# Low parts of weights: a subtraction on VectorE against a negated copy on ScalarE and an accumulating transfer

## The chip, the cores and the metric

The kernel runs on one core of a Trainium2 chip. The metric is the device time of one execution in microseconds (us), the median of the runs shown.

## The reference, cut to what matters

Two layers of a streaming encoder are computed for 512 prompt tokens and 64 sample tokens. Each layer has a combined input projection that feeds a gated convolution, two kinds of attention and three gates, a merge, an output projection, cross-attention into 256 memory tokens, and a gated MLP with a depthwise convolution:

```python
def layer(x, pos, lp, hist, mem_k, mem_v):
    g = lp['g_norms']
    m, new = token_mixers(rmsnorm(x, g[0]), pos, lp, hist)
    x = x + rmsnorm(m, g[1])
    c = cross_attention(rmsnorm(x, g[2]), mem_k, mem_v, lp['w_ca_q'], lp['w_ca_o'])
    x = x + rmsnorm(c, g[3])
    f, ffn_state = conv_ffn(rmsnorm(x, g[4]), lp['w_up'], lp['ffn_conv_w'], lp['w_down'], hist['ffn'])
    x = x + rmsnorm(f, g[5])
```

All inputs are float32. D_MODEL is 1024, D_FF is 2816.

## The kernel before, in words

Activations are held with features on the 128 partitions and the 576 tokens along the free dimension, in two halves of 288 (`HALF`). Every float32 operand of a matrix product is split into a high part (rounded to fp32r) and a low part (what the rounding left), and a product is three fp32r matmuls: high by high, low by high, high by low (`mm3`, L152). PE therefore runs three matmuls per tile of 128 by 128 weights and half of the tokens.

Weights come from memory through `load_w` (L137). It takes up to 1024 columns at a time into a buffer `raw` (three buffers of 1024 columns, `RAW` = 3), a load issued on SP (L143). For each piece of 512 columns or less it takes a pair of tiles, `wh` and `wl` (ten of each, `WH` = 10). ScalarE (ACT) copies the raw weight into `wh` with rounding (L130, by the helper at L123), and VectorE (DVE) writes raw minus high into `wl` (L131, by the helper at L126). There are 674 such pieces in the program. Nearly all dense products use a tile of 1024 columns, which is two pieces, eight steps of 128 along the contraction; 48 matmuls use it. The down projection (`down`, L1246) runs in five stages per layer, of four or five steps; its tiles have 512 or 640 columns, so that a five-step tile is one full piece and one of 128 columns.

The order of the instructions on each engine is written by a scheduler when the program is built, and each engine then executes its own list in that order. POOL holds the squares of the first norm (L227), the sums of the merge (L1086), half of the sums of squares (L243), the reciprocal square roots of the norms (L276), the residual sums (L329), the small copies of the convolution's edges (L951, L952, L955, L956) and a few transfers. DVE holds the evacuations of PSUM that are multiplied by something, the conv taps, and the low parts. ACT holds the plain evacuations, exponentials, squares, the Gelu, and the high parts.

The program begins with the input norm, the memory keys and values of both layers, and the cached latents (`begin`, L958), then goes through forgetting attention, latent attention, merge, cross-attention and MLP of layer 0, and the same of layer 1.

Of the kernel before, what the change touches and what calls it, by code (L numbers as in the profile page):

```python
# [15 lines left out]
F32 = mybir.dt.float32  # L16
F32R = mybir.dt.float32r
BF16 = mybir.dt.bfloat16
AF = mybir.ActivationFunctionType
ALU = mybir.AluOpType  # L20
# [4 lines left out]
P = 128  # L25
# [10 lines left out]
CONV_AT = {11: (0,), -1: (1,), 0: (2,), 2: (3,)}  # L36
ORDER = "xwh0ltcbnLmM"
GEARLY, FEARLY = 3, 2
RAW, WH = 3, 10
LAT_AT, MEM_AT = (1,), ((0, 1), (), ())  # L40
STAGES, NACT = ((0, 4), (4, 9), (9, 14), (14, 18), (18, 22)), 14
APOOL, XPOOL, OPOOL = (0, 1, 2, 3), (0, 1, 2, 3, 4), (0, 1, 2, 3, 4)
# [19 lines left out]
class Kernel:  # L62
# [74 lines left out]
    def load_w(self, ap, cols):  # L137

        pieces = []
        for c0 in range(0, cols, 1024):  # L140
            n0 = min(1024, cols - c0)
            raw = self.raw.tile([P, 1024], F32, tag="raw", name="raw")
            self.nc.sync.dma_start(raw[:, :n0], ap[:, c0:c0 + n0])  # L143
            for c in range(0, n0, 512):
                n = min(512, n0 - c)
                hi = self.wp.tile([P, 512], F32R, tag="wh", name="wh")
                lo = self.wp.tile([P, 512], F32R, tag="wl", name="wl")
                self.split(hi[:, :n], lo[:, :n], raw[:, c:c + n])
                pieces.append((hi, lo))
        return Weights(pieces)  # L150

# [1337 lines left out]
```

## Time and profile before

| what | us |
|---|---|
| median of two runs | 2537.87 (2537.53 to 2538.21) |
| the profiled execution, its own time | 2537.41 |
| its span, first to last instruction | 2535.3 |

The profile is of one execution. PE is TensorE's matmuls, PEld its weight loads, DVE is VectorE, ACT ScalarE, POOL GpSimd, SP SyncE. A line such as L123 is often a helper's, so the tile names say which of its uses is meant. "Idle before" is the time an engine stood still just ahead of a group, with what ended it. DMA shares are the mean busy share of the 16 DMA engines.

### The profile page before, as it was taken

How to read it: one execution, taken by the hardware profiler on the slowest of the kernel's cores; microseconds unless marked ns; L12 is line 12 of the kernel's file. 1: busy time of each engine (PE TensorE's matmuls, PEld its weight loads, DVE VectorE, ACT ScalarE, POOL GpSimd, SP SyncE). 2: the span in 40 equal slices, each digit the busy share in tenths (PEclk: the TensorE clock that was granted, in tenths of full speed). 3: DMA queues.
4: the chain of work that ended last, by engine and by line, in shares of the span. 5: the costliest groups of instructions: out<-in, count | busy, mean ns of one | idle time of the engine just before them, and what ended most of it. 6: DMA issues, size and time to landing. Idle time of an engine off the chain costs nothing. (4 is left out here: it accounts for less than half of the span.)

```text
span 2535.3 us, 45273 instructions
## 1 busy us (share of the span) xinstructions
PE 2418.0 (95%) x17478; PEld 2320.8 (92%) x17478; DVE 1576.6 (62%) x3249; ACT 1143.4 (45%) x2479; POOL 403.6 (16%) x723
## 2 busy tenths in 40 slices
PE   6999999999999999999989999999999899999997
PEld 6888897899998899999987889889999889999997
DVE  7757768644436675566676677774453767566565
ACT  4556545533345543333345554553233564433332
POOL 4000021002221421011130001100121323101012
PEclk9999999999998899999988999999999999999998
DMA  6763143333222032322233223323233202222321
GB/s 226 233 188 98 59 134 100 113 102 102 84 98 90 28 101 63 101 71 84 78 98 103 96 71 108 121 89 122 88 103 113 87 23 87 86 90 62 93 84 52
DMA packets 97510, 249.10 MB, mean 98 GB/s; under 512 B 12520, under 2 KB 26920, under 8 KB 97104
## 3 DMA queue, kind: packets, MB, share of 16 engines
q1 hardware_dynamic: 88880, 230.67, 29.4%
q0 software_dynamic: 3296, 8.54, 1.2%
q10 hardware_dynamic: 5120, 7.00, 0.8%
q8 instruction: 138, 2.26, 0.4%
q14 instruction: 76, 0.62, 0.1%
HBM read 206.18 MB, written 30.94 MB: 94 GB/s over the span
## 5 line engine op out<-in xcount | busy, mean ns | idle before, releaser
L123 ACT ACTIVATE wh<-raw 128x512 fp32r<-128x512 f32 (+2 forms) x674 | 405.1, 612 | 663.3 <-PE ps_S L156 300.9
L126 DVE TENSOR_TENSOR wl<-raw,wh 128x512 fp32r<-128x512 f32 (+2 forms) x674 | 444.7, 668 | 251.8 <-ACT wh L123 239.6
L155 PE MATMUL ps_d<-hh,wh 128*128 128x288 f32 (+1 forms) x1672 | 503.9, 301 | 0.8 <-DVE qbd L135 0.5
L157 PE MATMUL ps_d<-hh,wl 128*128 128x288 f32 (+1 forms) x1672 | 503.1, 301 | 0.0
L156 PE MATMUL ps_d<-hl,wh 128*128 128x288 f32 (+1 forms) x1672 | 502.1, 300 | 0.0
L156 PE MATMUL ps_S<-hl,wh 128*128 128x288 f32 (+1 forms) x1256 | 372.7, 297 | 0.4 <-DVE hl L285 0.4
L155 PE MATMUL ps_S<-hh,wh 128*128 128x288 f32 (+1 forms) x1256 | 371.7, 296 | 1.2 <-ACT hh L123 1.2
L157 PE MATMUL ps_S<-hh,wl 128*128 128x288 f32 (+1 forms) x1256 | 371.7, 296 | 0.0
L155 PEld LDWEIGHTS ps_d<-hh,wh 128*128 128x128 f32 (+1 forms) x1672 | 319.2, 191 | 3.3 <-issue 1.4
L157 PEld LDWEIGHTS ps_d<-hh,wl 128*128 128x128 f32 (+1 forms) x1672 | 319.0, 191 | 1.6 <-DVE wl L126 0.3
L156 PEld LDWEIGHTS ps_d<-hl,wh 128*128 128x128 f32 (+1 forms) x1672 | 319.2, 191 | 1.3 <-issue 0.2
L155 PEld LDWEIGHTS ps_S<-hh,wh 128*128 128x128 f32 (+1 forms) x1256 | 235.5, 188 | 2.8 <-ACT hh L123 1.8
L156 PEld LDWEIGHTS ps_S<-hl,wh 128*128 128x128 f32 (+1 forms) x1256 | 235.5, 187 | 1.5 <-DVE hl L285 0.6
L157 PEld LDWEIGHTS ps_S<-hh,wl 128*128 128x128 f32 (+1 forms) x1256 | 235.1, 187 | 0.6
L1086 POOL TENSOR_TENSOR mf<-mf,tm 128x288 f32<-128x288 f32 x64 | 64.4, 1006 | 451.4 <-DVE tm L1085 451.4
L955 POOL COPY fst<-u 128x2 f32<-128x2 f32 x88 | 32.2, 366 | 472.6 <-DVE u L319 472.6
L155 PE MATMUL ps_S<-ah,wh 128*128 128x288 f32 x352 | 105.6, 301 | 0.4 <-DVE m L1257 0.4
L156 PE MATMUL ps_S<-al,wh 128*128 128x288 f32 x352 | 105.8, 301 | 0.0
L157 PE MATMUL ps_S<-ah,wl 128*128 128x288 f32 x352 | 105.1, 299 | 0.0
L155 PE MATMUL ps_d<-ah,wh 128*128 128x288 f32 x352 | 104.0, 295 | 1.0 <-ACT ah L123 0.9
L157 PE MATMUL ps_d<-ah,wl 128*128 128x288 f32 x352 | 103.9, 295 | 0.0
L156 PE MATMUL ps_d<-al,wh 128*128 128x288 f32 x352 | 103.9, 295 | 0.0
(500 smaller groups left out, 5810.5 us busy)
## 6 DMA issues: line engine op xcount, KB each, us to landing
raw<-in_w_dram SPq DMA_DIRECT2D x250, 512.0 KB
raw<-in_down_dram SPq DMA_DIRECT2D x48, 256.0 KB
raw<-in_down_dram SPq DMA_DIRECT2D x32, 320.0 KB
of<-o_scr SPq DMA_DIRECT2D x24, 288.0 KB
x<-in_xT_dram SPq DMA_DIRECT2D x16, 288.0 KB
o_scr<-of SPq DMA_DIRECT2D x16, 288.0 KB
raw<-in_ukv_dram SPq DMA_DIRECT2D x8, 512.0 KB
kc_scr<-k SPq DMA_DIRECT2D x8, 512.0 KB
```

The lines of the kernel that those rows point to most:

```text
L123: self.nc.scalar.activation(out, in_, func, scale=scale, **k)
L126: self.nc.vector.tensor_tensor(out, a, b, op=ALU.subtract)
L155: mm(ps, w[0], x[0], start=first, stop=False)
L156: mm(ps, w[0], x[1], start=False, stop=False)
L157: mm(ps, w[1], x[0], start=False, stop=last)
L955: self.nc.gpsimd.tensor_copy(dst[:, 0:2], u[:, 512:514])
L1086: nc.gpsimd.tensor_tensor(mf[j][:, a:b], mf[j][:, a:b], tm[:, a:b], op=ALU.add)
```

## The change

`load_w` no longer fills a buffer of 1024 columns for two pieces. Each piece of up to 512 columns has a buffer of its own (tag `neg`, four of them) and a load of its own. ACT writes the negated, rounded weight into `wl` and the rounded weight into `wh`. Then a transfer issued on POOL adds the raw weight to `wl` in SBUF, element by element. DVE has no part in it. `RAW` goes from 3 to 1: the buffer of 1024 columns stays for two small constant loads. In SBUF the raw buffers take 12 KB per partition before and after.

```diff
-RAW, WH = 3, 10
+RAW, WH = 1, 10
...
         for c0 in range(0, cols, 1024):
             n0 = min(1024, cols - c0)
-            raw = self.raw.tile([P, 1024], F32, tag="raw", name="raw")
-            self.nc.sync.dma_start(raw[:, :n0], ap[:, c0:c0 + n0])
             for c in range(0, n0, 512):
                 n = min(512, n0 - c)
                 hi = self.wp.tile([P, 512], F32R, tag="wh", name="wh")
                 lo = self.wp.tile([P, 512], F32R, tag="wl", name="wl")
-                self.split(hi[:, :n], lo[:, :n], raw[:, c:c + n])
+                raw = self.raw.tile([P, 512], F32, tag="neg", name="raw", bufs=4)
+                self.nc.sync.dma_start(raw[:, :n], ap[:, c0 + c:c0 + c + n])
+                self.act(lo[:, :n], raw[:, :n], scale=-1.0)
+                self.act(hi[:, :n], raw[:, :n])
+                self.nc.gpsimd.dma_start(lo[:, :n], raw[:, :n].bitcast(F32R), accum_op=ALU.add)
                 pieces.append((hi, lo))
```

Two lines are added ahead of most of the file, so L276 of before is L278 after, and so on. The order of the instructions changes on every engine. Three places show it.

POOL at the start of the program, before. `sq` and `acc` are squares of the input and their sums, `r` is the reciprocal root of a norm, `mt` the memory tokens:

```order
L227 TENSOR_TENSOR acc<-x 128x288
L227 TENSOR_TENSOR sq<-x 128x288 x7
L276 TENSOR_TENSOR r<-s,negh 96x3
L227 TENSOR_TENSOR sq<-x 128x288 x5
L384 TENSOR_TENSOR acc<-mt 128x256
```

and after:

```order
L229 TENSOR_TENSOR acc<-x 128x288
L229 TENSOR_TENSOR sq<-x 128x288 x4
L150 DMA wl<-raw 128x320
L229 TENSOR_TENSOR sq<-x 128x288 x3
L278 TENSOR_TENSOR r<-s,negh 96x3
L150 DMA wl<-raw 128x512 x3
L229 TENSOR_TENSOR sq<-x 128x288 x4
L386 TENSOR_TENSOR acc<-mt 128x256
```

The accumulating transfers stand among the squares of the first norm.

POOL in the merge of layer 0, where `mf` is the merged sum and `pacc` a sum of squares. Before:

```order
L897 DMA vs<-vc_scr_108 128x1024
L1086 TENSOR_TENSOR mf<-mf,tm 128x288 x32
L243 TENSOR_TENSOR pacc<-pacc,sq 128x288 x7
```

and after (the pattern goes on to the end of the merge):

```order
L1047 DMA out_conv_dram<-cst 128x16
L150 DMA wl<-raw 128x512 x31
L1088 TENSOR_TENSOR mf<-mf,tm 128x288 x2
L150 DMA wl<-raw 128x512 x3
```

Three transfers now stand between two pairs of sums.

ACT in the MLP of layer 0, from the end of one pair of up tiles into the first stage of the down projection; `ah` is the activated product, `y` the conv output, `m` the output of the down projection. Before:

```order
L123 ACTIVATE ah<-at 128x576
L123 ACTIVATE wh<-raw 128x512 x2
L123 ACTIVATE y<-u,fprm 128x578
L123 ACTIVATE wh<-raw 128x512 x2
L123 ACTIVATE y<-y 128x578
L123 ACTIVATE y<-u,fprm 128x578
L123 ACTIVATE m<-ps_d 128x288
```

and after:

```order
L123 ACTIVATE ah<-at 128x576
L123 ACTIVATE wh<-raw 128x512
L123 ACTIVATE wl<-raw 128x512
L123 ACTIVATE wh<-raw 128x512
L123 ACTIVATE wl<-raw 128x512
L123 ACTIVATE y<-u,fprm 128x578
L123 ACTIVATE wh<-raw 128x512
L123 ACTIVATE wl<-raw 128x512
L123 ACTIVATE wh<-raw 128x512
L123 ACTIVATE y<-y 128x578
L123 ACTIVATE y<-u,fprm 128x578
L123 ACTIVATE m<-ps_d 128x288
```

Each high part now has a negated copy beside it, ahead of the conv taps, the Gelu and the evacuations.

## Rows read from the trace of the kernel before

**Rows 1.** The page, part 1: busy time, share, instructions per engine.
```profile
PE 2418.0 (95%) x17478; PEld 2320.8 (92%) x17478; DVE 1576.6 (62%) x3249; ACT 1143.4 (45%) x2479; POOL 403.6 (16%) x723
```

**Rows 2.** Busy time by stretch: stretch, its length, then engines, clock, DMA share.
```profile
core 0: us, PE busy (x) PEld busy (x) DVE busy (x) ACT busy (x) POOL busy (x), PEclk, DMA share, GB/s
0.00:190.00 190.00, 160.93 (x1134) 148.47 (x1135) 128.42 (x255) 98.07 (x203) 32.23 (x39) 0.99 0.66 216
507.00:697.00 190.00, 190.00 (x1436) 190.00 (x1435) 87.87 (x162) 64.91 (x121) 30.26 (x30) 1.00 0.31 96
887.00:1268.00 381.00, 381.00 (x2878) 380.69 (x2878) 237.42 (x461) 142.42 (x237) 52.31 (x165) 1.00 0.28 83
1775.00:1902.00 127.00, 127.00 (x960) 127.00 (x960) 59.55 (x109) 43.02 (x80) 25.92 (x26) 1.00 0.30 94
2092.00:2471.00 379.00, 376.81 (x2833) 376.37 (x2834) 238.84 (x465) 142.94 (x242) 60.01 (x177) 1.00 0.28 84
```

**Rows 3.** The same stretches, DVE's instructions on `wl` alone, with their number.
```profile
0.00:190.00 190.00, 44.78 (x67) 0.99 0.66 216
507.00:697.00 190.00, 41.45 (x60) 1.00 0.31 96
887.00:1268.00 381.00, 85.15 (x135) 1.00 0.28 83
1775.00:1902.00 127.00, 27.64 (x40) 1.00 0.30 94
2092.00:2471.00 379.00, 82.81 (x132) 1.00 0.28 84
```

**Rows 4.** Groups of instructions, page part 5: the high and low parts of weights.
```profile
L123 ACT ACTIVATE wh<-raw 128x512 fp32r<-128x512 f32 (+2 forms) x674 | 405.1, 612 | 663.3 <-PE ps_S L156 300.9
L126 DVE TENSOR_TENSOR wl<-raw,wh 128x512 fp32r<-128x512 f32 (+2 forms) x674 | 444.7, 668 | 251.8 <-ACT wh L123 239.6
```

**Rows 5.** PE's waits: total us, times, longest.
```profile
PE ps_T L255 <- DVE acc L243: 35.6, 11, 17.0
PE ps_n L271 <- DVE nd L264: 7.1, 10, 1.7
```

**Rows 6.** ACT in order of time, MLP of layer 0: start, us, what, idle before.
```profile
909.82 0.63 ACT L123 ACTIVATE wh<-raw 128x512 fp32r<-128x512 f32 x1 [1.21 <-PE ps_S L156]
911.42 0.63 ACT L123 ACTIVATE wh<-raw 128x512 fp32r<-128x512 f32 x1 [0.97 <-PE ps_S L156]
...
922.54 0.63 ACT L123 ACTIVATE wh<-raw 128x512 fp32r<-128x512 f32 x1 [2.47 <-PE ps_S L156]
...
935.26 0.63 ACT L123 ACTIVATE wh<-raw 128x512 fp32r<-128x512 f32 x1 [2.46 <-PE ps_S L156]
...
1052.57 1.16 ACT L123 ACTIVATE wh<-raw 128x512 fp32r<-128x512 f32 x2 [2.78 <-PE ps_d L156]
1056.55 1.16 ACT L123 ACTIVATE wh<-raw 128x512 fp32r<-128x512 f32 x2 [2.83 <-PE ps_S L156]
```

**Rows 7.** POOL's groups: busy us, mean ns of one, idle before.
```profile
L1086 POOL TENSOR_TENSOR mf<-mf,tm 128x288 f32<-128x288 f32 x64 | 64.4, 1006 | 451.4 <-DVE tm L1085 451.4
L955 POOL COPY fst<-u 128x2 f32<-128x2 f32 x88 | 32.2, 366 | 472.6 <-DVE u L319 472.6
L276 POOL TENSOR_TENSOR r<-s,negh 96x3 f32<-96x3 f32 x24 | 23.2, 968 | 101.5 <-DVE s L258 101.5
L897 POOL DMA_DIRECT2D vs<-vc_scr x8 | 4.5, 557 | 7.3 <-PE ps_o L564 7.2
```

**Rows 8.** DMA queue of SP in 887 to 1268 us: packets, MB, share of 16 engines.
```profile
q1 hardware_dynamic: 11232, 31.10, 27.7%
```

**Rows 9.** SP's waits: total us, times, longest.
```profile
SPq L143 <- DVE wl L126: 1612.3, 320, 39.6
```

**Rows 10.** SP and ACT in order of time near 25 us: one load and its use.
```profile
24.83 0.33 SPq L143 DMA_DIRECT2D raw<-in_ukv_dram  x1
...
28.35 1.15 ACT L123 ACTIVATE wh<-raw 128x512 fp32r<-128x512 f32 x2 [1.28 <-DMA raw<-in_ukv_dram]
```

**Rows 11.** DMA issues, page part 6: number, KB each, median us from issue to landing.
```profile
vs<-vc_scr POOLq DMA_DIRECT2D x8, 512.0 KB, 4.7
qr<-rh POOLq DMA_DIRECT2D x16, 64.0 KB, 2.5
```

## The prediction

> **What bounds the kernel now.** I read the page's engine shares first, then the busy times by stretch, the groups of instructions, the waits, and the DMA views last. PE is busy 2418.0 of 2535.3 us [rows 1]: all idle time of PE together is 117 us. By stretch [rows 2] the up and down projections of both layers (887 to 1268 and 2092 to 2471 us) and the merges (507 to 697, 1775 to 1902) leave PE nothing or 2 us; the first 190 us lose 29 us. DVE is busy 62% and ACT 45%, and neither bounds a stretch. So taking work from DVE can win at most what PE now waits for DVE, while anything that makes weights arrive late in the full stretches is lost time. The demand for weights, in pieces of 512 columns, is one low part made on DVE each: 67 in the first 190 us, 135 and 132 in the two stretches of up and down projections, 60 and 40 in the merges [rows 3], one per 2.8 to 2.9 us in those three stretches and one per 3.2 us in the merges. The DMA engines are 66% busy in the first 190 us and 28 to 31% in the other four [rows 2].
>
> **What goes.** 674 subtractions on DVE of 668 ns, 445 us [rows 4]. PE's longest wait for DVE is the sum of squares, 35.6 us, 17.0 of it one wait at the start, where DVE alternates with POOL squares; the next is 7.1 us [rows 5]. Of these I give the change 13 us: DVE stands between them with few low parts, but a shorter queue helps every boundary. Bounds: 0 and 43 us (both rows whole).
>
> **What ACT gets.** 674 more copies of 612 ns [rows 4], 412 us, so ACT goes from 1143 to 1556 us, 61%. In the five-tile stage of the down projection ACT spends 1.16 us on the two high parts of a tile and waits 2.8 of 3.98 us, and in a pair of up tiles it waits 0.97 us between two high parts [rows 6]: the copies fit in these gaps and I cost them at nothing. If a copy waits for a late load, though, what is queued behind it on ACT waits too: evacuations of PSUM, the conv taps and the Gelu, and for these PE waits within a few tiles. That is priced below as a late ring.
>
> **What POOL gets.** 674 transfers to issue. The nearest row is a 512 KB load issued from POOL, 557 ns [rows 7]: 375 us, POOL from 404 to 779 us, 31%. Each now stands in POOL's order behind and ahead of other work, and each waits for ACT's copy. In the merges three of them stand between two sums of 1006 ns; in the start they stand among the squares that PE's first 17 us wait needs; at the boundaries they stand ahead of the reciprocal root. I take 0.56 us for each of the 24 roots [rows 7], 13 us, which cancels the 13 us won on DVE. Bounds: 0 and 40 us (three transfers ahead of each root).
>
> **What the DMA engines get.** Loads are now 2 KB rows instead of 4 KB, and 256 KB is moved a second time, from SBUF to SBUF, with an addition. No accumulating transfer is in this trace. A plain packet in 887 to 1268 us takes 0.277 x 381 x 16 / 11232 = 150 ns for 2769 bytes [rows 8], an estimate of 111 ns for 2 KB; eight rows per engine make 0.89 us of all 16 engines per piece. An addition reads source and destination and writes one result, where a copy reads and writes once. So I bound it by 1 copy (the second read is free) and 3 copies (both reads and the write one after the other): 0.89 to 2.67 us. I take 2 copies, 1.78 us, the middle. With 135 - 16 x 0.75 = 123 full pieces (16 of the 135 are quarter pieces of 128 columns) the up and down stretch goes from 28% to 28 + 57 = 86% busy (57% at one copy, 114% at three). The first 190 us go from 66% to 66 + 63 = 129% (97% and 160%): 55 us more transfer time than there is. Not every transfer there is waited for (caches are written to memory for later), so I take half, +28 us. Bounds: 0 and 114 us.
>
> The Trainium skill has a rule that speaks against this change: "Collectives: The Full Stack", in the section on the bandwidth ceiling, says that an addition in the transfer runs at about half the rate of a copy, since it needs two source reads on the same ring. No run here shows it yet. By the plain packet of the trace the time would stay near the rival A below, by that rule it would be the forecast.
>
> **The ring of raw buffers.** Before, three buffers of 1024 columns were free again when DVE had subtracted; SP waited 1612.3 us for that [rows 9], so loads ran well ahead. Now four buffers of 512 columns are free when the accumulating transfer has landed. One turn of a buffer: issue on SP 0.33 us; load. A 512 KB load issued at 24.83 us was used at 28.35, 3.5 us [rows 10], and a 64 KB transfer lands in 2.5 us [rows 11], so by a line between them 2.9 us for 256 KB; copy on ACT 0.61; issue on POOL 0.56; the accumulate. POOL's transfers land in 2.5 us at 64 KB and 4.7 at 512 KB [rows 11]: 3.4 us at 256 KB, of which 1.26 is data, counted twice 4.7. Sum 9.1 us. One operation ahead on ACT (0.61) and two copies ahead on POOL (2 x 366 ns [rows 7]) make 10.5. With the engines 86% busy I let the load find one accumulate ahead (1.78) and the accumulate one load (0.89): 13.1 us for four pieces. (At one copy 11.0 by the same sum, at three 15.3.)
>
> The budget: in pairs of up tiles four pieces per 12.72 us (high parts at 909.82, 922.54 and 935.26 us [rows 6]); in the five-tile down stages two tiles, two full and two quarter pieces, per 7.96 us (1052.57 to 1056.55 is one tile [rows 6]). So the ring is late by 0.4 us per pair: 44 pairs, 18 us. In a five-tile stage quarter pieces turn in an estimated 10.5 us, the mean is 11.8, the ring is late by 3.8 us per two tiles, 15 us per stage, 61 us in the four stages. Ten pieces lie ready, five tiles or 20 us of that stage, and hide part where the pairs have filled them again; I take half, 30 us. Bounds for both: 0 (ring at 11.0 us in pairs, its lag in the down stages hidden) to 180 us (15.3 us: 2.6 x 44 = 114, and 66 for the stages).
>
> Attention needs no term: its stretches use a piece in 5 to 6 us by my estimate from 674 less the 434 pieces of rows 3 over the other 1268 us [rows 3, 4]. What waits on SP behind a raw load there (keys, queries and cached values) is issued in the same queue as before.
>
> **Sum.** 2537.4 us (the profiled execution: its span of 2535.3 and 2.1 around it, 0.5 below the median of the two runs) - 13 + 13 + 28 + 18 + 30 = 2613 us.
>
> **Rivals.** A: the accumulate costs a copy. For it: SBUF to SBUF needs no memory access, and 256 KB is small beside the 28% share. Then the ring turns in 11.0 us inside 12.72, DMA is 57% busy, and the start is just at 97%: 2537 - 13 + 13 + about 3 = 2540 us, not slower. It decides from the point where a turn is under 12.7 us. B: the accumulate costs three copies or more, and DMA becomes the bound: 14% over in 381 us and 13% in 379 (+53, +47), 15% and 14% in the merges (+29, +18), half of 114 at the start (+57): 2741 us. For it: both reads and the write pass the same 16 engines; against it: reads and writes can overlap. C: faster. PE's waits for DVE shrink by both rows of 43 us and POOL's part costs nothing: 2494 us; to pass 2% (51 us) more waits would have to go as well. Against it: the order on PE is fixed when the kernel is built, and the 17 us wait hangs on POOL's squares too. D: the change does not take DVE's place (PE waits for low parts as often as for DVE): that needs a wait of PE for low parts, of which the trace has nearly none; it is part of B.
>
> **How the numbers follow.** Forecast 0.45 (2560 to 2690, one tenth of all chances in its part below 2%), A 0.33, B 0.17, C 0.03, small effects of either sign 0.02. A measurement of this kernel tells about 2% from no change: slower 0.35 + 0.17 = 0.52, within 0.10 + 0.33 + 0.02 = 0.45, faster 0.03. The range leaves out the low end of A and C and the far end of B: 2525 to 2750 us.
>
> **What would show it.** Right: ACT's copy to the low part waits for raw loads in the up and down stretches, SP waits for the accumulating transfers, PE shows idle time there (now 0 and 2 us), DMA above 80% in them, and the first 190 us of work end later by some 30 us. Wrong: the q0 queue's packets near 111 ns for 2 KB and PE still full in the up and down stretches (A), or the DMA share at its ceiling with landings far over 5 us (B). POOL issues of 1 us or more in place of 0.56 would move the late point from the DMA engines to POOL, a step that my sum has as small.

## The result, and the profile after

The changed kernel takes 2687.26 us (median of two runs, 2686.43 to 2688.09), the kernel before 2537.87: 149 us more, a ratio of 1.059 with a 95% interval of 1.054 to 1.063. It is slower, and the forecast of 2613 us had the right direction with half of the size. The profiled execution of the changed kernel spans 2686.3 us, 151.0 more than before.

The page's part 1 after, which answers to [rows 1]:

```profile
PE 2477.4 (92%) x17478; PEld 2376.6 (88%) x17478; DVE 1178.4 (44%) x2575; ACT 1459.8 (54%) x3153; POOL 916.1 (34%) x1397
```

DVE lost 398 us of work, and it won nothing. PE's idle time, span less busy, went from 117.3 to 208.9 us (+91.6), and the same 17478 matmuls took 59.4 us longer. Both parts have to be explained. The stages tell where they lie. The next two fences are busy times by stretch, in the columns of [rows 2], with the limits set at the same events in both kernels: the first and the last exponential of a layer's attention (tile `p`), the first high part of the merged sum (`mh`), and the first and last convolution of the MLP (`y`). Before:

```profile
0.00:177.00 177.00, 150.31 (x1071) 140.75 (x1072) 118.49 (x231) 90.22 (x181) 32.23 (x39) 0.99 0.70 229
177.00:471.00 294.00, 277.41 (x1938) 251.33 (x1938) 220.72 (x514) 166.60 (x437) 27.82 (x51) 1.00 0.33 98
...
636.00:893.00 257.00, 244.59 (x1696) 235.47 (x1696) 140.49 (x289) 124.50 (x297) 66.36 (x80) 0.92 0.23 74
893.00:1273.00 380.00, 380.00 (x2869) 380.00 (x2868) 237.18 (x459) 143.89 (x238) 53.20 (x169) 1.00 0.29 86
...
1375.00:1698.00 323.00, 304.30 (x2104) 275.72 (x2104) 230.51 (x533) 173.26 (x449) 29.13 (x55) 0.99 0.31 95
```

After:

```profile
0.00:224.00 224.00, 164.49 (x1041) 152.56 (x1042) 79.67 (x164) 121.24 (x241) 79.89 (x102) 0.86 0.95 247
224.00:545.00 321.00, 289.85 (x1973) 263.64 (x1974) 187.83 (x460) 195.10 (x496) 75.27 (x108) 0.96 0.57 139
...
714.00:984.00 270.00, 245.35 (x1688) 235.86 (x1687) 110.83 (x233) 151.39 (x354) 108.38 (x136) 0.91 0.55 126
984.00:1362.00 378.00, 378.00 (x2855) 378.00 (x2853) 159.38 (x323) 200.92 (x370) 148.10 (x298) 1.00 0.79 169
...
1473.00:1823.00 350.00, 316.02 (x2111) 287.37 (x2111) 192.37 (x471) 203.20 (x512) 80.47 (x117) 0.94 0.56 135
```

The start is 47 us longer with the DMA engines at 0.95. Each attention stage is 27 us longer, though its DMA share is only 0.57. The MLP, with a DMA share of 0.79 and nearly three times the work on POOL, is not longer at all. In the first attention stage PE idles 31.2 us in place of 16.6 (321 - 289.85 and 294 - 277.41), and it is busy 12.4 us longer. Of these, some 5 us are an estimate for 35 more matmuls in the stage, at the mean of 143 ns before (277.41 / 1938); 30 fewer lie in the start. The other 7 us go with a mean granted clock of 0.96 in place of 1.00.

PE's waits after, which answer to [rows 5]: total us, times, longest.

```profile
PE ps_S L770 <- DMA k<-k: 39.3, 8, 12.5
PE ps_T L257 <- DVE acc L245: 36.5, 10, 17.0
PE ps_S L157 <- ACT p L1144: 19.5, 2, 10.1
PE ps_S L923 <- DMA k<-k: 17.0, 8, 3.6
```

The same three groups before:

```profile
PE ps_S L155 <- ACT p L1142: 3.9, 2, 1.9
PE ps_S L921 <- DMA k<-k: 2.8, 3, 1.5
PE ps_S L768 <- DMA k<-k: 1.4, 4, 0.6
```

Two kinds of wait have grown most. The larger is for `k<-k`. A key is made on half of the partitions and then copied to the other half by a transfer from SP's queue (L741 in forgetting attention, L913 in latent attention), and the score matmul reads it next. PE waits 56.3 us for these copies, 4.2 before. In the first attention stage they make 16.3 us (0.7 before), about as much as PE's idle time grew there, 14.6 us; in the second, 21.3 us (2.7 before), where it grew by 15.3. The smaller is for the first exponentials of cross-attention (`p`, L1144), 10.1 and 9.4 us between merge and MLP, 1.9 each before.

The longest of the waits for a key, as the chain of waits tells it (start, us, what; stretch from 200 to 240 us of the changed kernel):

```profile
203.30 5.93 DMA raw<-in_wv_dram
...
210.93 5.80 DMA wl<-raw
...
216.79 0.33 SPq L147
...
217.22 5.74 DMA k<-k
...
223.09 0.55 PE ps_S L770
```

In the chain a raw load takes 5.93 us, the accumulating transfer that follows it 5.80. SP's next raw load, at 216.79, needs the buffer that this frees, and the key copy stands behind it in SP's queue. Then the key copy itself takes 5.74 us. PE had nothing to do from 210.6 to 223.1 us. What that does to PE's clock is in stretches of 4 us of the same execution:

```profile
212.00:216.00 4.00, 0.00 (x0) 0.00 (x0) 2.20 (x4) 3.95 (x8) 0.95 (x2) 0.63 0.93 216
216.00:220.00 4.00, 0.00 (x0) 0.00 (x0) 0.00 (x0) 1.95 (x3) 1.64 (x2) 0.50 1.08 239
220.00:224.00 4.00, 0.91 (x4) 0.84 (x5) 0.00 (x0) 0.00 (x0) 0.00 (x0) 0.50 0.97 256
224.00:228.00 4.00, 4.00 (x20) 3.48 (x21) 1.36 (x4) 2.27 (x7) 0.86 (x1) 0.67 0.06 21
228.00:232.00 4.00, 4.00 (x33) 3.67 (x31) 2.67 (x9) 3.68 (x11) 0.86 (x1) 1.00 0.73 182
```

While PE has no work the granted clock falls to 0.50, the 1.2 GHz level, and it is back at 1.00 only from 228 us. In the timeline of PE a score matmul of the same line and shape, 128x256, takes twice as long just behind that wait as at the full clock:

```profile
223.09 0.55 PE L770 MATMUL ps_S<-k,q 128*128 128x256 f32 x1 [12.47 <-DMA k<-k]
...
228.84 0.28 PE L770 MATMUL ps_S<-k,q 128*128 128x256 f32 x1
```

So a wait for a key can cost itself and then a stretch of matmuls at the lower level. Cut into stretches of 6 us, the first attention stage shows a granted clock under 0.97 only beside PE's waits that end at 223, 300, 332, 458 and 531 us, four of them for keys. A wait for a key of 2.7 us that ends at 255 us shows no fall.

The other wait, for the exponentials of cross-attention, in the chain ahead of its end at 892.04 us (start, us, what):

```profile
876.50 7.65 DMA wl<-raw
884.21 3.86 DMA raw<-in_w_dram
...
890.97 1.03 ACT p L1144 x4
```

SP's next raw load waits for the buffer that this accumulating transfer frees. ACT's copies of that load start at 888.18 us, and the exponentials stand behind them in ACT's order. This is the late ring that the prediction feared, in cross-attention and not in the MLP.

Last, what the accumulating transfer and its issue cost: the queue (packets, MB, share), the landing (number, KB each, median us) and the group of the issues, against [rows 7, 8, 11].

```profile
q0 software_dynamic: 100352, 177.99, 39.1%
wl<-raw POOLq DMA_DIRECT2D x632, 256.0 KB, 4.3
L150 POOL DMA_DIRECT2D wl<-raw x674 | 587.4, 883 | 1398.4 <-ACT wl L123 1221.9
```

3296 of the packets and 1.2% of 2535.3 us were on this queue before. The rest is (0.391 x 2686.3 - 0.012 x 2535.3) x 16 / 97056 = 168 ns a packet, and with 97056 / 674 = 144 packets a transfer 1.51 us of all 16 engines per piece. The issue takes 883 ns on POOL, where 557 was assumed.

### The profile page after: what moved, and what is told of

It is laid out like the page before. It is cut to its first block, busy times and chain, and to the rows that moved or that the text cites. A ratio compares the mean times of both kernels' runs of the same rounds, so it can differ in the third digit from the quotient of the medians.

```text
span 2686.3 us, 47586 instructions
## 1 busy us (share of the span) xinstructions
PE 2477.4 (92%) x17478; PEld 2376.6 (88%) x17478; DVE 1178.4 (44%) x2575; ACT 1459.8 (54%) x3153; POOL 916.1 (34%) x1397
## 4 chain that ended last, share of the span: by engine, by line
PE 65%; DMA 10%; issue 9%; DVE 6%; ACT 5%; POOL 3%; SPq 0%; POOLq 0%; ACTq 0%; DVEq 0%
PE ps_d L158 10%; PE ps_d L157 10%; PE ps_d L159 10%; PE ps_S L157 9%; PE ps_S L158 9%; PE ps_S L159 8%; DMA wl<-raw 3%; DMA raw<-in_w_dram 3%; DMA k<-k 2%; DVE hl L287 1%; POOL wl L150 1%; PE ps_T L509 1%; ACT wl L123 1%; DVE x L331 1%; PE ps_T L257 1%
## 5 line engine op out<-in xcount | busy, mean ns | idle before, releaser
L150 POOL DMA_DIRECT2D wl<-raw x674 | 587.4, 883 | 1398.4 <-ACT wl L123 1221.9
L157 PE MATMUL ps_d<-hh,wh 128*128 128x288 f32 (+1 forms) x1672 | 509.3, 305 | 3.9 <-ACT wh L123 3.6
L158 PE MATMUL ps_d<-hl,wh 128*128 128x288 f32 (+1 forms) x1672 | 508.2, 304 | 0.0
L123 ACT ACTIVATE wl<-raw 128x512 fp32r<-128x512 f32 (+2 forms) x674 | 403.1, 600 | 98.7 <-DMA raw<-in_w_dram 58.0
L948 DVE SCALAR_TENSOR_TENSOR y<-u,fprm,y 128x578 f32<-128x578 f32 x88 | 72.3, 821 | 127.1 <-ACT y L123 126.9
L474 DVE TENSOR_REDUCE nm<-ps_S 128x1 f32<-128x128 f32 (+3 forms) x128 | 62.1, 490 | 138.0 <-PE ps_S L493 81.6
L475 ACT ACTIVATE p<-ps_S,nm 128x128 f32<-128x128 f32 (+3 forms) x128 | 67.1, 525 | 87.9 <-DVE nm L474 79.2
```

Of the source, the lines that this page charges most:

```text
L123: self.nc.scalar.activation(out, in_, func, scale=scale, **k)
L150: self.nc.gpsimd.dma_start(lo[:, :n], raw[:, :n].bitcast(F32R), accum_op=ALU.add)
L157: mm(ps, w[0], x[0], start=first, stop=False)
L158: mm(ps, w[0], x[1], start=False, stop=False)
L474: nc.vector.tensor_reduce(nm[:, i:i + 1], S, axis=AX.X, op=ALU.max, negate=True)
L475: nc.scalar.activation(p, S, AF.Exp, bias=nm[:, i:i + 1], scale=1.0, accum_out=sums[:, i:i + 1])
```

## Experiments

The theories on record: 1, the ring of four buffers is late; 2, the traffic on the DMA engines makes other transfers on the chain late; 3, ACT's added copies and the order they force; 4, POOL's issues; and, for the last runs, 5, key copies stuck behind raw loads in SP's queue. This table has the profiled execution of each kernel by stages, both layers together, as differences from before (us, limits as above; "merge to MLP" runs from the last exponential to the first convolution; what lies behind the last convolution, 45 us, is left out and changes by 1.1 us at most). Each row is one execution, and the eight executions of e1 lie between 2533 and 2546 us; matmuls can also fall on the other side of a limit, as the 35 above. Differences of a few us are not told apart.

| kernel | to the first exponential | attention | merge to MLP | MLP | MLP to attention | span |
|---|---|---|---|---|---|---|
| before | 177.2 | 615.5 | 837.0 | 757.9 | 102.9 | 2535.3 |
| after | +47.2 | +54.3 | +42.6 | -0.8 | +8.1 | +151.0 |
| e1 | +4.9 | -2.4 | -1.2 | -0.5 | -1.5 | -0.4 |
| e2 | -3.2 | +11.9 | +19.5 | +0.1 | +1.5 | +29.9 |
| e3 | +48.3 | +42.5 | +33.4 | -0.5 | +6.7 | +129.9 |
| e4 | +43.6 | +60.9 | +30.5 | -0.8 | +8.1 | +141.9 |
| e5 | +26.8 | +36.5 | +28.4 | -0.8 | +3.4 | +94.2 |
| e6 | +14.7 | +4.0 | +15.1 | -0.5 | +1.3 | +34.1 |
| e7 | +36.2 | +25.9 | +33.1 | -0.9 | -1.6 | +92.8 |
| e8 | +5.6 | +9.0 | +19.7 | -0.6 | -1.0 | +32.1 |
| e9 | +20.0 | +61.9 | +35.7 | -0.8 | +7.7 | +123.4 |
| e10 | +45.9 | +44.6 | +33.8 | -0.8 | +11.3 | +134.4 |
| e11 | +3.2 | +16.5 | +0.8 | -0.3 | +6.7 | +27.0 |
| e12 | +17.3 | +47.4 | +0.8 | -0.6 | +7.7 | +72.8 |

**e1: the new loads and buffers, with the subtraction on DVE.** Against after:

```diff
-                self.act(lo[:, :n], raw[:, :n], scale=-1.0)
-                self.act(hi[:, :n], raw[:, :n])
-                self.nc.gpsimd.dma_start(lo[:, :n], raw[:, :n].bitcast(F32R), accum_op=ALU.add)
+                self.split(hi[:, :n], lo[:, :n], raw[:, :n])
```

> The changed kernel's loads and its four raw buffers of 512 columns, but the low part made by the subtraction on DVE as before: no negated copy, no accumulating transfer. Theory 1 (the late ring: a raw buffer comes free only when the accumulating transfer has landed, and what stands behind the raw loads on SP and behind the copies on ACT is late): a buffer is free 1.3 us after its load, so 2540 us, between 2530 and 2560. Theory 2 (contention: the second transfer slows every other one): no second transfer, 2540 us. Rival, the loads themselves: 2 KB rows and a ring a third shorter cost most of the loss, 2620 us or more, with the loss at the start and in attention still there.

Measured 2537.58 us, ratio 1.0017 (0.9995 to 1.0039). Loads of 2 KB rows and four buffers of 512 columns cost nothing as long as DVE frees them. PE's waits show a second thing:

```profile
PE ps_T L255 <- DVE acc L243: 22.0, 11, 5.5
PE ps_d L155 <- ACT wh L123: 14.2, 1, 14.2
```

The 17.0 us wait at the start [rows 5] is gone here, with DVE's work the same, and no time is won by it: a wait of 14.2 us for a high part stands at the start in its place.

e1 also gives the measure for the key copies, since it has the time and the traffic of before and its chain of waits reaches through the whole program. The key copies on that chain in the first attention stage of e1 (start, us):

```profile
205.03 2.87 DMA k<-k
...
245.65 2.73 DMA k<-k
...
273.01 2.84 DMA k<-k
...
423.59 2.64 DMA k<-k
...
462.62 2.40 DMA k<-k
```

and in the same stage of the changed kernel:

```profile
294.17 5.28 DMA k<-k
...
327.39 4.42 DMA k<-k
...
416.08 2.48 DMA k<-k
...
455.75 5.10 DMA k<-k
...
487.18 4.53 DMA k<-k
```

Five in each; the mean goes from 2.70 to 4.36 us. The share of the DMA engines, in stretches of 3 to 6 us around the five, is 0.63 to 0.80 in e1. In the changed kernel it is 0.97 to 1.09 around four, and 0.63 around the copy at 416 us, which takes 2.48 us. The transfer itself is slower where the accumulating ones fill the engines.

**e2: the kernel before with ACT's negated copy added**, which DVE then overwrites:

```diff
+        self.act(lo, src, scale=-1.0)
         self.act(hi, src)
         self.sub(lo, src, hi.bitcast(F32))
```

> The kernel before with one more copy on ACT per piece: the negated raw weight into the low part, which DVE then overwrites as before. It adds 674 x 0.61 = 412 us to ACT and nothing to the DMA engines. Theories 1 and 2: these fit in ACT's gaps, 2540 us, at most 2565. Theory 3 (ACT: the added copies delay exponentials and evacuations, and the order that the scheduler writes is worse): 2600 us or more, with the loss in attention and cross-attention.

Measured 2568.26 us, ratio 1.0138 (1.0108 to 1.0167), 34 us, between the two ranges expected. The loss is in attention (12 us) and between merge and MLP (20 us). In the MLP the copies are free, as predicted; in these two stages they are not. Of the 12 us, some 6 are again more matmuls in the first attention stage, 1978 in place of 1938. That ACT's own work stands between PE's products there is the likely reason and was not tested by itself.

**e3: the traffic alone.** e1, with an accumulating transfer of the same size for each piece, from the high part into one of two tiles that nothing reads (here, in e6 and in e7 the two constant loads use the small buffers too, which makes room):

```diff
                 self.split(hi[:, :n], lo[:, :n], raw[:, :n])
+                self.dn += 1
+                dst = self.dummy[self.dn % 2]
+                self.nc.gpsimd.dma_start(dst[:, :n], hi[:, :n], accum_op=ALU.add)
```

> The first kernel of this call (DVE subtracts) with one accumulating transfer of 256 KB per piece that nothing waits for: it adds the high part to one of two scratch tiles. It puts the same traffic on the DMA engines and the same 674 issues on POOL, but no raw buffer is held by it and no low part hangs on it. Theory 1: the start loses up to 30 us, elsewhere little, 2570 us at most. Theory 2: 2640 us or more, the loss spread over start and attention as in the changed kernel.

Measured 2670.09 us, ratio 1.0539 (1.0509 to 1.0570). 674 transfers that no matmul waits for cost 133 us more than e1, nearly the whole loss, and in the same stages. PE waits 27.3 us for key copies (16.9 and 10.4) though no low part depends on POOL. So most of the loss is not lateness of the low parts. Column by column, e2 and e3 together give the changed kernel's start (45.1 of 47.2) and attention (54.4 of 54.3): of the loss in attention the traffic makes about 42 us and ACT's copies about 12.

**e4: six buffers in place of four** (the two constant loads use them too, so that they fit):

```diff
-                raw = self.raw.tile([P, 512], F32, tag="neg", name="raw", bufs=4)
+                raw = self.raw.tile([P, 512], F32, tag="neg", name="raw", bufs=6)
```

> The changed kernel with six raw buffers in place of four (the room comes from the two constant loads, which now use these buffers). Theory 1: SP's waits for accumulating transfers shrink and a third to two thirds of the loss outside the start goes, 2610 to 2650 us, with the waits of PE for keys (39 and 17 us) halved. Theory 2: the traffic is the same, 2680 us. Theory 3: 2680 us.

Measured 2682.14 us, ratio 1.0587 (1.0556 to 1.0618): no different from after. Theory 1 falls as the account of the loss. It is not without a trace: PE's wait for the exponentials of cross-attention is 7.0 us in place of 19.5, and merge to MLP is 12 us shorter, but attention is 7 us longer.

**e5: a plain transfer for the accumulating one.** The low part is then the raw weight: the addition is left out.

```diff
-                self.nc.gpsimd.dma_start(lo[:, :n], raw[:, :n].bitcast(F32R), accum_op=ALU.add)
+                self.nc.gpsimd.dma_start(lo[:, :n], raw[:, :n].bitcast(F32R))
```

> The changed kernel with the addition left out of the transfer: the raw weight is copied over the negated one, so the low part holds the raw weight. Same loads, copies on ACT, issues on POOL, waits and rows; only the second read of the destination goes. Theory 2 (traffic on the DMA engines makes the other transfers on the chain late): a transfer takes 0.9 us of the engines in place of 1.5, so 40% of the 133 us that the unread transfers cost goes, 2635 us (2610 to 2660). Theory 4 (POOL: 0.88 us per issue, rows per transfer, what waits behind it there): the issues are the same, 2675 to 2690 us.

Measured 2624.74 us, ratio 1.0341 (1.0279 to 1.0403), as theory 2 expected. The queue, the landing and the issue of this kernel:

```profile
q0 software_dynamic: 100352, 177.99, 22.6%
wl<-raw POOLq DMA_DIRECT2D x632, 256.0 KB, 2.7
L150 POOL DMA_DIRECT2D wl<-raw x674 | 363.2, 539 | 1513.3 <-ACT wl L123 1296.6
```

Worked out as above, a packet takes (0.226 x 2629.5 - 0.012 x 2535.3) x 16 / 97056 = 93 ns, 0.84 us of all engines per piece. The addition makes that 1.51 us, the landing 4.3 instead of 2.7, the issue 883 instead of 539 ns, and it costs 2.5% of the time, 62 us. The other 87 us of the loss are there with a plain copy.

**e6: e3 with 32 columns in each transfer** instead of 512, so that issues and packets stay and the bytes go:

```diff
-                self.nc.gpsimd.dma_start(dst[:, :n], hi[:, :n], accum_op=ALU.add)
+                self.nc.gpsimd.dma_start(dst[:, :32], hi[:, :32], accum_op=ALU.add)
```

> The kernel in which DVE subtracts and an unread accumulating transfer runs beside it, with that transfer cut from 512 columns to 32: as many issues and rows, one sixteenth of the bytes. Theory 2, by bytes: 2560 us at most. Theory 4: POOL's issue time goes by rows, so 0.8 to 0.9 us per issue and 2640 us or more.

Measured 2570.31 us, ratio 1.0127 (1.0097 to 1.0156), 10 us over theory 2's range and far below theory 4's. Its landing and its issue:

```profile
dummy<-wh POOLq DMA_DIRECT2D x674, 16.0 KB, 3.2
L155 POOL DMA_DIRECT2D dummy<-wh x674 | 589.7, 891 | 1234.7 <-ACT wh L127 985.8
```

The issue takes 891 ns whatever the size. Issues and packets together cost 28 us against e1 by the ratios, 33 by the medians, mostly at the start and between merge and MLP; the queue of the packets alone is 8.9% of the engines, so this is not POOL's price alone. The bytes cost the other 100 us of e3, at the start, in attention (42.5 against 4.0) and between merge and MLP. The key copies follow: five on the chain in the first attention stage of e6 take 3.10 us in the mean, five in e3 4.83.

**e7: traffic without POOL.** e1 with two stores of the high part to memory for each piece, issued on ACT:

```diff
+                for _ in range(2):
+                    self.dn += 1
+                    self.nc.scalar.dma_start(self.dump[self.dn % 32][:, :n], hi[:, :n].bitcast(F32))
```

> The kernel in which DVE subtracts, with two plain stores of each high part to memory that nothing reads, issued on ACT: about 1.8 us of the DMA engines per piece, none of it through POOL. Theory 2: 2650 us or more, with keys late as in the changed kernel. Theory 4: what the 1348 issues cost on ACT, 20 to 60 us, 2560 to 2600 us, and keys at 2.5 to 3 us.

Measured 2624.46 us, ratio 1.0340 (1.0289 to 1.0392). A queue of 37.6% of the engines, near the 38.2% of e3, costs 82 us more than e1 by the ratios, 87 by the medians, with no added issue on POOL, and key waits appear again (14.7 and 7.7 us). It lies between the two ranges expected. ACT's 1348 issues of 327 ns are in that number too, so it is no clean price of the traffic.

**e8: the change in the merges and MLPs alone**, 432 of the 674 pieces; elsewhere the subtraction on DVE from the same buffers. A switch in `load_w` chooses, and e9 and e12 use it too:

```diff
+                if self.accum:
...
+                else:
+                    self.split(hi[:, :n], lo[:, :n], raw[:, :n])
...
+                    self.accum = True
                     mhl = self.merge(l, h, pool)
+                    self.accum = False
...
+                    self.accum = True
                     self.ffn(l, h, m, xs, finish, pool)
+                    self.accum = False
```

> The change in the merges and the MLPs alone, 434 - 67 = 367 pieces and the few at their edges; all other weights go through the same four buffers with the subtraction on DVE. The trace of the changed kernel has PE without idle time there, so 2540 to 2555 us: the 149 us hang on the other pieces. If the late ring or the traffic costs something in these stretches too, 2580 us or more.

Measured 2572.86 us, ratio 1.0137 (1.0101 to 1.0173), 35 us. I had expected less. None of it lies inside the MLP, whose own stage is unchanged with the 267 pieces of [rows 3] in it; 19.7 us lie between merge and MLP. In each layer 11 of its accumulating transfers are issued before the last exponential, from 422.7 us on in layer 0, and attention is 9.0 us longer.

**e9: the change everywhere but in the beginning of the program**, 627 pieces:

```diff
+        self.accum = False
         h = self.new_h()
...
         self.nsq = 3
+        self.accum = True
         return st["bias"]
```

> The kernel after, except that the weights used in the beginning of the program (input norm, memory keys and values, cached latents) are split by a copy on ACT and a subtraction on DVE as before, from the same four buffers of 512 columns; the accumulating transfer makes all other low parts. If the 47 us lost ahead of the first exponential are a loss of the start alone, the time is 2687 - 47 = 2640 us (2632 to 2648). If what is late at the start only waits for the same DMA traffic, and part of it is lost again further on (the late start hides some of the late keys of layer 0), it is 2650 to 2670. If the start is not limited by the transfers at all (ACT's copies or POOL's issues cost it only a little), the first exponential comes at 215 us or later and the time stays above 2675.

Measured 2655.23 us, ratio 1.0474 (1.0455 to 1.0493). The first exponential comes at 197.2 us, 27 us earlier than after, and 7.6 us of that are lost again in attention. 47 pieces are worth about 30 us. This is the second of the three cases expected; the 14 accumulating transfers that are left ahead of the first exponential belong to attention's first weights.

**e10: the key and query copies on ACT's queue** in the changed kernel (five lines, all of this form):

```diff
-                    nc.sync.dma_start(k[o].bitcast(F32), k[r].bitcast(F32))
+                    nc.scalar.dma_start(k[o].bitcast(F32), k[r].bitcast(F32))
```

> The kernel after, with the transfers of attention operands (key and query halves, bias rows) issued on ACT's queue, where their inputs are made, and no longer on SP behind loads of raw weights. Theory 5 (head of line: a raw load on SP waits for a buffer that an accumulating transfer has not yet freed, and the key transfer waits behind it): PE's waits for the key transfers (39.3 and 17.0 us) fall below 20 us together, and the time falls by 20 to 40 us, 2647 to 2667. Theory 2 (the DMA engines are full and the transfer itself is slow): the waits stay near 50 us and the time is 2680 to 2695. Third: the key transfers' issue on ACT, some 0.5 to 1 us each, holds back copies and exponentials queued behind it: 2690 to 2720.

Measured 2668.43 us, ratio 1.0527 (1.0507 to 1.0548), its interval only just touching that of after. PE's waits for keys over the whole program, in this kernel:

```profile
PE ps_S L770 <- DMA k<-k: 19.6, 6, 6.1
...
PE ps_S L923 <- DMA k<-k: 15.1, 7, 3.0
```

They fall from 56.3 to 34.7 us, not below 20. In the first attention stage they are 14.6 us (6.4 and 8.2) where they were 16.3, and the stage is 318.8 us long where it was 320.2. Ahead of the first exponential the wait of 12.5 us is 3.8 here, as SP's queue in the chain above would have it, yet that stretch is only 1.3 us shorter. The waits inside attention stay when the queue is another. Neither theory's ranges are met in full: the time is 1 us over theory 5's, the waits are between.

**e11: the same move in the kernel before**, the same five lines:

```diff
-                    nc.sync.dma_start(q2[q][64:68].bitcast(F32), bl[r].bitcast(F32))
+                    nc.scalar.dma_start(q2[q][64:68].bitcast(F32), bl[r].bitcast(F32))
```

> The kernel before, with the same transfers of attention operands issued on ACT's queue in place of SP's. The control for the run above: PE waits 4 us for key transfers there, so by theory 5 there is nothing to win, 2533 to 2542 us. If the issue on ACT costs its queue something, it shows here without the accumulating transfers: 2545 to 2565 us.

Measured 2562.59 us, ratio 1.0104 (1.0085 to 1.0122): 28 us slower, so the second expectation holds. The move itself costs ACT's queue something, and what e10 shows is a net number. How the two add up was not taken further.

**e12: the change in forgetting and latent attention alone**, 130 pieces:

```diff
+            self.accum = True
             self.fox(l, h, bias, self.o_scr[l][1])
         self.mla(l, h, self.o_scr[l][2])
+        self.accum = False
```

> The change only in forgetting attention and latent attention of both layers (with the gated convolution that lies among them); the start, the merges, cross-attention and the MLPs split on DVE as before, from the same four buffers of 512 columns. The prediction gave this part nothing: then 2537 us, at most 2548. If the loss of the changed kernel sits here as its stages show it (27 us more in each of the two attention stages), the time is 2537 + 54 = 2591 us (2580 to 2605), with the two stages near 320 and 349 us and the other stages as before. If the attention stages are late only because weights, keys and POOL are already behind when they begin (after the start, after the MLP), they fall back to within 10 us of before each, and the time is 2540 to 2560.

Measured 2606.33 us, ratio 1.0275 (1.0257 to 1.0294). A fifth of the pieces makes half of the loss, 72 us, 1 us over the range expected if the loss sits in attention. The attention stages are 318.7 and 344.2 us long (after: 320.2 and 349.6); the two columns at +17.3 and +7.7 hold the first weights of each layer's attention, 14 and 17 pieces, which are made ahead of its first exponential. Merge, cross-attention and MLP are as before. The first attention stage of this kernel has the same shape as after's:

```profile
185.00:500.00 315.00, 284.19 (x1900) 256.68 (x1899) 186.28 (x448) 188.69 (x475) 68.28 (x99) 0.95 0.54 136
```

and so have PE's waits:

```profile
PE ps_S L773 <- DMA k<-k: 27.9, 8, 6.3
...
PE ps_S L926 <- DMA k<-k: 12.6, 7, 3.2
```

Attention's loss comes with the accumulating transfers of its own weights; it is not carried in from those of the start or of the MLP.

## Why the prediction was right in direction and short by half

**The step that failed** is "Attention needs no term": I compared the rate at which that stage uses weights with the rate at which they arrive, and said of the key copies only that they are issued in the same queue as before. The two attention stages lost 54.3 us, and e12 shows 72 with the weights ahead of them. About 12 of the 54 are ACT's copies (e2), about 42 the traffic (e3), and 4 are left when its bytes go (e6). Weights are made ahead, ten pieces lie ready, and a late one is hidden. A key copy can't be made ahead: ACT writes the key, the transfer moves it, PE reads it. Its own duration stands in the chain, and with the accumulating transfers on the same 16 engines that duration grew. It went from 2.70 to 4.36 us (e1 and after, above). A mean DMA share of 0.57 said nothing against this: in stretches of 6 us the share of that stage goes from 0.00 to 1.08, and it was 0.97 to 1.09 around the four slow copies.

**The late ring, +18 and +30,** cost nothing in the MLPs, where it was priced. Both MLP stages are 0.8 us shorter together. ACT does wait for raw loads there, as predicted, in the MLP of layer 0 for up to 5.30 us; one such wait:

```profile
1156.98 0.63 ACT L123 ACTIVATE wh<-raw 128x512 fp32r<-128x512 f32 x1 [4.92 <-DMA raw<-in_w_dram]
```

PE stays full over it: the ten ready pieces, about 28 us of PE's work at one per 2.8 us, are more than such a wait. The ring was late elsewhere, in cross-attention, where the exponentials stand behind ACT's copies: PE's wait there went from 3.9 to 19.5 us, and is down to 7.0 with six buffers (e4) and 8.6 where no buffer waits for the transfers (e3). The prediction named this way ("what is queued behind it on ACT waits too") and priced it for the MLPs alone. The sum of a turn also counts SP's issue twice: the 3.5 us of a load, from 24.83 to 28.35 us [rows 10], hold its 0.33 us already. Without it a turn is 12.8 us, and the 18 us shrink to an estimated 4. That I let the ten ready pieces hide half of a stage's lag and none of the pairs' was too little. Without these 48 us, and with attention at nothing, the sum would have been 2565 us: the forecast came as near as it did by luck, because an error in one place stood in for an omission in another.

**The start, +28,** measured 47. With 32 columns (e6) 14.7 us of it remain, and 48.3 with the full traffic (e3), so the bytes make some 34, not far from the half of 55 that was taken. What the sum lacked there is the cost of issues and packets. e9 gives back 27 of the 47.

**ACT's copies, costed at nothing,** are free in the MLP, from which I took the gaps [rows 6], and cost 34 us in e2, most of it between merge and MLP and in attention. The gaps of one stage were carried to the others.

**POOL, +13,** was mis-sized: 883 ns an issue instead of 557, and 28 to 33 us in e6, packets included, instead of 13. **DVE, -13,** brought nothing: PE's wait for the sum of squares is 36.5 us, 17.0 the longest, as it was [rows 5], and in e1, where the long one is gone, the time is the same.

**The accumulating transfer itself** was sized well: 1.51 us of the engines for 1.78 assumed, 0.84 for a copy where 0.89 was assumed, 4.3 us to land for 4.7, a DMA share of 0.79 in the MLP for 0.86. The Trainium skill ("Collectives: The Full Stack", the section on the bandwidth ceiling) says of collectives that a transfer with an addition runs at about half the rate of a copy, since it reads two sources. These runs agree for the engine time: 1.51 against 0.84 us, 1.8 times. Of the rivals, A had the MLP right and nothing else; B, DMA as the bound, comes near the rows at the start alone, where the share is 0.95.

The parts add to more than the whole: 133 us (e3 over e1) and 34 (e2) against 149. Of the 133, some 30 are issues and packets and 100 bytes. By stages the two add up at the start and in attention; between merge and MLP, +42.6 us, copies (19.5), issues (15.1) and bytes (33.4 less 15.1) overlap. PE's wait for the exponentials makes 15.6 us there; which cost ends last at the other boundaries stays open.

## What to carry to other kernels

That the DMA engines have room on average does not make it free to move elementwise work into transfers: look for the small transfers whose result the next matmul needs, and charge each with the longer duration; the MLPs, which run through a store of ready tiles, showed nothing. A wait of PE behind which the granted clock falls costs more than its own length, so count it with the matmuls behind it. Where a buffer comes free late, look also at what stands behind the copy that waits for it on its engine. And ask first whether the engine that is relieved ends any wait: 398 us less work on DVE was worth nothing here.

## What the runs showed of the hardware that was not expected

The issue of an accumulating transfer on POOL takes 883 to 891 ns with 512 or 32 columns, that of a plain one 539: it hangs on the addition here, not on the bytes. At 16 KB an accumulating transfer still takes 3.2 us to land, at 256 KB 4.3, and the plain copy of 256 KB 2.7. In the wait at 210 us the granted clock was at 0.50 for at least 8 us, and the first matmuls behind it took 0.55 us for 0.28.
